# A gate chain on 32 rows, retention tiles normalised in pairs, and earlier loads in attention, in a two-layer mLSTM and retention trunk

## The chip, the cores and the metric

The kernel runs on one core of a Trainium2 chip. A core has a matrix engine (PE, with PEld for its weight loads), VectorE (DVE), ScalarE (ACT), GpSimd (POOL) and SyncE (SP), whose queue issues most DMA transfers. The metric is the device time of one execution in microseconds; lower is better.

## The reference

Two layers, each with 1024 tokens of width 1024. A layer normalises x, applies an adaptive scale and shift, projects it to queries, keys, values and gates, and runs eight heads of width 256: four mLSTM heads and four retention heads. Both kinds of head are chunked linear attention with a carried state. Cut to what matters here:

```
# mLSTM head, per chunk; li = input gate, lf = log_sigmoid(forget gate)
b = cumsum(lf);  a = b + m
g = b[:, None] - b[None, :] + li[None, :]          (causal)
m_row = max(a, max(g));  s = (q k^T) * exp(g - m_row)
h = (s v + exp(a - m_row) * C q) / max(|den|, exp(-m_row))
# retention head: s = (q k^T) * gamma^(t-s);  o = s v + gamma^(t+1) q R
# both: per-head layer norm over 256 columns, gates, y @ w_out, residual
```

The gate chain is the part that makes cumulative sums b, a running maximum of li - b, and sums of these, for every head and token, before any mLSTM head runs. Running sums and maxima restart in each layer and go over all 1024 tokens.

## The kernel before, in words

Products are made from split operands (a high part rounded to the matrix engine's fp32r format and a low part), three matmuls for one (`mm3`, lines 177 to 179 of the profile). Projections run as a list of slots: pairs of blocks in a Strassen-like scheme, with weights fetched by a `Feeder` seven or eight slots ahead into a ring of twelve tiles `R`, split by `high` (L403, ACT) and `low` (L408, POOL or DVE). Value products have 256-column matmuls, the others 512.

Beside the slots run generators, in ticks: one tick per slot (or per half block in the units before them). `launch(gen, delay)` starts a generator, and what it yields is the number of ticks until its next part. A tick only sets the place of instructions in the program. PE's order is the program's order (`manual_schedule`). The other engines' order is made by a scheduler that simulates the program in time; instructions marked `late` keep their program order among themselves. In the gate chain all DVE calls are marked so.

The gate chain (`gate_chain`) starts one tick after the gate projection. Before, it works on rows 0 to 3 (forget gate, four heads) and 32 to 35 (input gate), in two halves of 512 tokens, one after the other, with the last column of a half as the start of the next. ACT makes |f|, exp and ln; then 12 ticks; then DVE makes log-sigmoid, splits it into a coarse and a fine part, scans both (`bq`, `br`), and scans the maximum (`mx`). It collects four results in rows 0, 32, 64 and 96 of a tile `T4`; eight 128x128 transposes by PE (L562) and two copies give the column form `COL`. The maxima also go to DRAM (`mdr`), from where attention later loads decay rows, broadcast over the partitions. The chain takes the tiles `q`, `kc`, `dm`, `nd`, `cf`, `n`, `zt`, `cH`, `cL`, which attention and the rotary tables also use. `load_rotary` (L968) loads two sine tables into `dm`, with a buffer ring of two, and one into `nd`.

Attention (`attention`) handles one head in four chunks j of 256 tokens. `TABLE` gives one step for each tick: `q0` and `k0` load queries and keys of chunk 0 from DRAM into tiles `acc` (a ring of twelve, which nearly everything else uses too), `Q0` and `K0` split them (ACT L868, POOL L869), `d0` loads the decay rows of an mLSTM head into `dm` (ring of two), `m0` turns them into weights (POOL L1021, ACT L1022), `t0` loads key rows (four transfers, L905), `s0` splits them, `v0` loads values into `ring`, `S0` makes scores (L1032, then DVE L1048 to L1062, ACT L1070 for `sH`, POOL L1071 for `sL`), `V001` makes outputs of tiles 0 and 1 of chunk 0 (L1114 at chunk 0, L1123 for later chunks), and `U01` updates the state (L1091, L1094, L1096). At step 22 the next head may start.

After `values` (V), `normalise` makes the layer norm of a head. For mLSTM it runs once per chunk. For retention it runs, before, once for each V step: `V001` covers both tiles, but chunks 1 to 3 have two V steps, so each tile has its own statistics (L1160, L1161), added epsilon (L1174), power -0.5 on POOL (L1175), `nmu` (L1178) and scaling on ACT (L1180). `finish` then transposes both tiles into `zt` (L1188, one buffer) and stores them (L1193). Retention's unnormalised outputs are copied into `n` (L1144, one buffer).

Of the kernel before, what the change touches and what calls it, by code (L numbers as in the profile page):

```python
# [87 lines left out]
def tile_hybrid_trunk(ctx, tc, x, xt, c, positions, w_ada, b_ada, norm_g, w_in, w_blk, w_val, conv_w, conv_b,  # L88
# [27 lines left out]
    def ps_a():  # L116
        return pa.tile([P, 512], F32, tag="a", name=nm("pa"))
# [88 lines left out]
           for l in range(DEPTH)]  # L206
    gbd = [dpool.tile([P, HALF], F32, name=f"gbd{i}") for i in range(2)]
    mdr = [dpool.tile([NH, T], F32, name=f"mdr{l}") for l in range(DEPTH)]

    ring = [cst.tile([P, 4 * 258], F32R, tag=f"ring{i}", name=f"ring{i}") for i in range(2)]  # L210
    ring3 = [r.rearrange("p (a c) -> p a c", a=4) for r in ring]
# [291 lines left out]
    def gate_chain(l, pgs, gt):  # L503
        V = Later()
        bg = cols[l][1]
        COL = wt("COL", 8 * 16, 1)
        C4 = COL.rearrange("p (t k h) -> p t k h", t=8, k=4)
        prev = {}
        on4 = ones.to_broadcast([P, 512])
        lfs, lis_, es = [], [], []  # L510
        mxs, fbs, lif = wt("q", 1024, 2), wt("q", 1024, 2), wt("kc", 1024, 1)
        for half in range(2):
            pg = pgs[half]
            hs = slice(half * HALF, (half + 1) * HALF)
            fb, li, e = fbs[:, hs], lif[:, hs], wt("dm", 512, 2)
            A.activation(fb[0:4], pg[0:4, :], AF.Identity, bias=bg[0:4, :])
            A.activation(li[32:36], pg[32:36, :], AF.Identity, bias=bg[32:36, :])
            A.activation(e[0:4], fb[0:4], AF.Abs)
            A.activation(e[0:4], e[0:4], AF.Exp, scale=-1.0)
            lfs.append(fb)  # L520
            lis_.append(li)
            es.append(e)
        for half in range(2):
            A.activation(es[half][0:4], es[half][0:4], AF.Ln, bias=ones[0:4, 0:1])
        yield 12
        T4s = []
        for half in range(2):
            lf, li, e = lfs[half], lis_[half], es[half]
            lfq = (wt("cf", 516, 1) if half else wt("nd", 516, 1))[:, 0:512]
            V.scalar_tensor_tensor(lf[0:4], lf[0:4], 0.0, e[0:4], ALU.min, ALU.subtract)  # L530
            V.tensor_scalar(lfq[0:4], lf[0:4], MAG_Q, -MAG_Q, ALU.add, ALU.add)
            V.tensor_tensor(lf[0:4], lf[0:4], lfq[0:4], ALU.subtract)
            bq, br = e, wt("zt", 512, 1) if half else wt("n", 512, 1)
            yield 1
            V.tensor_tensor_scan(bq[0:4], on4[0:4], lfq[0:4], prev.get("bq", 0.0), ALU.mult, ALU.add)
            V.tensor_tensor_scan(br[0:4], on4[0:4], lf[0:4], prev.get("br", 0.0), ALU.mult, ALU.add)
            yield 1
            lir, T4, mx = li, wt("cL" if half else "cH", 516, 1)[:, 0:512], mxs[:, half * HALF:(half + 1) * HALF]
            liq, uh = lf, lfq
            V.tensor_scalar(liq[0:4], li[32:36], MAG_Q, -MAG_Q, ALU.add, ALU.add)  # L540
            V.tensor_copy(lir[0:4], li[32:36])
            V.tensor_tensor(lir[0:4], lir[0:4], liq[0:4], ALU.subtract)
            G.memset(T4, 0.0)
            V.tensor_tensor(uh[0:4], liq[0:4], bq[0:4], ALU.subtract)
            yield 1
            V.tensor_copy(T4[0:4], uh[0:4])
            V.tensor_tensor(T4[32:36], lir[0:4], br[0:4], ALU.subtract)
            V.tensor_tensor_scan(mx[0:4], on4[0:4], uh[0:4], prev.get("mx", 0.0), ALU.mult, ALU.max)
            yield 1
            V.tensor_copy(T4[64:68], mx[0:4])  # L550
            V.tensor_tensor(uh[0:4], bq[0:4], mx[0:4], ALU.add)
            V.tensor_tensor(T4[96:100], uh[0:4], br[0:4], ALU.add)
            Q.dma_start(mdr[l][:, half * HALF:(half + 1) * HALF], mx[0:4])
            prev = {"bq": bq[0:4, 511:512], "br": br[0:4, 511:512], "mx": mx[0:4, 511:512]}
            T4s.append(T4)
            yield 1
        yield 3
        for half in range(2):
            T4 = T4s[half]
            pt = ps_a()  # L560
            for i in range(4):
                PE.transpose(pt[:, i * P:(i + 1) * P], T4[:, i * P:(i + 1) * P], ident)  # L562
            V.tensor_copy(C4[:, half * 4:(half + 1) * 4],
                          pt.rearrange("p (t k h) -> p t k h", t=4, k=4)[:, :, :, 0:4])
# [24 lines left out]
        V.tensor_tensor(we, we, eul4[:, :, 0:6, 0], ALU.mult)  # L589
        gt.update(C4=C4, eul4=eul4, em3=em3, wi=wi, we=we, dc=dc)  # L590
# [372 lines left out]
    def load_rotary(rot):  # L963
        for which in range(2):
            for i in range(2):
# [3 lines left out]
                rot[which].append(t[:, 0:HALF])  # L969

    busy = [False]
    TABLE = ("q0 k0 d0 t0", "", "v0", "Q0 K0 m0 d1", "s0 k1", "S0", "m1 q1 K1", "v1", "Q1", "V001 t1", "S1 k2 q2", "U01",
             "s1 d2 K2", "v2 Q2", "V10 U2 m2", "S2", "t2 d3", "V11 U3 k3", "s2 q3", "v3 K3", "Q3 m3", "V20 U4",
             "S3", "", "V21 U5", "", "", "", "V30", "V31", "")
    RELEASE = 22

    def attention(l, hg, gt):
# [120 lines left out]
        def values(j, tts):  # L1098
# [6 lines left out]
            src = {}  # L1105
# [10 lines left out]
            for tt in tts:  # L1116
# [23 lines left out]
                    else:  # L1140
                        A.copy(nd3[:, tt, 0:W], po[:, 0:W])
                else:
                    src[tt] = nrm[j][:, tt, :]
                    A.copy(src[tt], po[:, 0:HD])  # L1144
            if not ml:
                launch(normalise(j, tts, src), 1)
            elif tts[-1] == 1:
                launch(normalise(j, (0, 1), [nd3[:, tt, 0:HD] for tt in range(2)]), 1)

        def gather(nd, po):  # L1150
            V.tensor_tensor(nd, po, nd, ALU.add)
            return
            yield

        def normalise(j, tts, src):
            n, a, b = len(tts), tts[0], tts[-1] + 1
            st6 = wt("st6", 12, 2)
            mv3 = wt("mv", 4, 2).rearrange("p (a b) -> p a b", a=2)
            for tt in tts:
                V.bn_stats(st6[:, 6 * tt:6 * tt + 6], src[tt])  # L1160
                V.bn_aggr(mv3[:, tt, :], st6[:, 6 * tt:6 * tt + 6])  # L1161
            va = wt("va", 2, 2)[:, 0:n]
            rs = wt("rsd", 2, 2)[:, 0:n]
            if ml:
                den = st["nd"][:, :, HD]
                r = wt("qd", 2, 2)
# [4 lines left out]
                G.tensor_tensor(rs, va, mhalf[:, 0:2], ALU.pow)  # L1171
            else:
                e = C_EPS + 2 * h + place(2 * j + a)
                V.tensor_tensor(va, mv3[:, a:b, 1], kc[:, e:e + n], ALU.add)  # L1174
                G.tensor_tensor(rs, va, mhalf[:, 0:n], ALU.pow)  # L1175
            yield 1
            nmu = wt("nmu", 2, 2)[:, 0:n]
            late(V.scalar_tensor_tensor(nmu, mv3[:, a:b, 0], -1.0, rs, ALU.mult, ALU.mult))  # L1178
            for i, tt in enumerate(tts):
                late(A.activation(nrm[j][:, tt, :], src[tt], AF.Identity, scale=rs[:, i:i + 1], bias=nmu[:, i:i + 1]))  # L1180
            if tts[-1] == 1:
                yield 1
                yield from finish(j)

        def finish(j):
            half = j // 2
# [530 lines left out]
```

## Time and profile before

| | before |
|---|---|
| median of 3 runs | 2268.21 us (2267.9 to 2268.85) |
| profiled execution | 2268.18 us |
| its span, first to last instruction | 2266.5 us |
| mean granted clock of the matrix engine | 0.979 |
| PE busy | 2151.5 us, 95% |
| DVE busy | 1817.5 us, 80% |
| ACT busy | 1159.4 us, 51% |
| POOL busy | 964.3 us, 43% |

The profile is one execution. Busy time of an engine is the time in which it had an instruction at work; for PE the matmuls overlap, so busy is not the same as full use. A wait is told as who waited, for whom, the total, how often, and the longest. The chain of waits is followed back from the last instruction, at each step to what released it. "Granted clock" is the share of full speed that PE's throttle gave.

### The profile page before, as it was taken

The page shows a single profiled execution, that of the slowest core. Times are in us where ns is not written, and L with a number is a line of the kernel's source. Part 1 is how long each engine was busy: PE and PEld are TensorE (multiplying, and loading weights), DVE is VectorE, ACT ScalarE, POOL GpSimd, SP SyncE. Part 2 cuts the span into 40 slices and gives each one's busy share as a digit, 9 for nine tenths or more (in the row PEclk, how much of TensorE's full clock was granted, in tenths as well). Part 3 has the DMA queues.
Part 4 walks back from the last instruction along what each step waited for, and adds up shares of the span by engine and source line. Part 5 has one row for each costly group of instructions (what it writes and reads, how often), then busy time and mean ns, then how long its engine had stood idle before and what let it go on. Part 6 is the DMA issues. An engine that isn't in the chain of part 4 may idle for free.

```text
span 2266.5 us, 35156 instructions
## 1 busy us (share of the span) xinstructions
PE 2151.5 (95%) x11483; PEld 1832.0 (81%) x11483; DVE 1817.5 (80%) x3205; ACT 1159.4 (51%) x2163; POOL 964.3 (43%) x842
## 2 busy tenths in 40 slices
PE   7988999999999999999999799999999899999998
PEld 5787789878898878788778678988987888788886
DVE  6899888989979998784738989788797889977653
ACT  7634345444565656553555434543565565655442
POOL 1443244445454454424366235544544453442313
PEclk9999999999999999999999899999999999999999
DMA  8266688787686777686633767776866686686974
GB/s 285 61 176 186 188 230 249 215 235 202 185 247 175 194 203 186 175 270 210 225 107 84 214 185 210 214 198 185 245 166 192 175 238 186 173 216 203 261 245 118
DMA packets 452549, 448.31 MB, mean 198 GB/s; under 512 B 191219, under 2 KB 309755, under 8 KB 452365
## 3 DMA queue, kind: packets, MB, share of 16 engines
q1 hardware_dynamic: 432636, 410.14, 58.9%
q0 software_dynamic: 19584, 35.66, 10.4%
q8 instruction: 90, 1.47, 0.3%
q14 instruction: 95, 0.77, 0.1%
q10 hardware_dynamic: 144, 0.26, 0.0%
HBM read 322.69 MB, written 123.24 MB: 197 GB/s over the span
## 4 chain that ended last, share of the span: by engine, by line
PE 57%; DVE 22%; DMA 10%; issue 5%; POOL 2%; ACT 2%; SPq 1%; DVEq 0%; POOLq 0%; ACTq 0%
PE px L177 8%; PE px L178 8%; PE px L179 8%; PE pz L179 6%; PE pz L178 6%; PE pz L177 6%; PE pa L177 4%; PE pa L179 4%; PE pa L178 4%; DVE acc L881 3%; DVE R L408 2%; PE pa L1123 2%; DVE acc L626 2%; DMA acc<-kfr 1%; PE pa L1032 1%
## 5 line engine op out<-in xcount | busy, mean ns | idle before, releaser
L403 ACT CAST wH<-R 128x512 fp32r<-128x512 f32 x616 | 377.2, 617 | 476.6 <-PE px L178 133.0
L408 POOL TENSOR_TENSOR R<-R,wH 128x512 fp32r<-128x512 f32 x276 | 397.5, 1447 | 479.5 <-ACT wH L403 325.9
L177 PE MATMUL px<-b,wH 128*128 128x512 f32 x912 | 364.8, 400 | 8.2 <-ACT acc L767 7.4
L179 PE MATMUL px<-b,R 128*128 128x512 f32 x912 | 365.7, 401 | 0.0
L178 PE MATMUL px<-b,wH 128*128 128x512 f32 x912 | 364.8, 400 | 0.0
L408 DVE TENSOR_TENSOR R<-R,wH 128x512 fp32r<-128x512 f32 x340 | 257.2, 760 | 90.5 <-ACT wH L403 87.5
L178 PE MATMUL pz<-b,wH 128*128 128x512 f32 x704 | 280.2, 398 | 1.3 <-DVE b L1262 1.3
L179 PE MATMUL pz<-b,R 128*128 128x512 f32 x704 | 281.0, 399 | 0.0
L177 PE MATMUL pz<-b,wH 128*128 128x512 f32 x704 | 279.8, 397 | 0.2 <-ACT acc L767 0.2
L177 PEld LDWEIGHTS px<-b,wH 128*128 128x128 f32 x912 | 174.6, 191 | 48.1 <-ACT acc L767 8.9
L179 PEld LDWEIGHTS px<-b,R 128*128 128x128 f32 x912 | 174.0, 191 | 42.0 <-POOL R L408 0.8
L178 PEld LDWEIGHTS px<-b,wH 128*128 128x128 f32 x912 | 174.4, 191 | 39.3
L177 PE MATMUL px<-wH,b 128*128 128x256 f32 (+1 forms) x576 | 177.7, 309 | 27.4 <-DVE acc L824 12.3
L178 PE MATMUL px<-R,b 128*128 128x256 f32 (+1 forms) x576 | 174.9, 304 | 3.7 <-DVE R L408 3.7
L179 PE MATMUL px<-wH,b 128*128 128x256 f32 (+1 forms) x576 | 175.8, 305 | 0.0
L701 POOL DMA_DIRECT2D R<-in_w_blk_dram x104 | 92.1, 886 | 185.3 <-DMA R<-in_w_blk_dram 90.8
L178 PEld LDWEIGHTS pz<-b,wH 128*128 128x128 f32 x704 | 133.5, 190 | 32.0 <-DVE b L1262 2.2
L179 PEld LDWEIGHTS pz<-b,R 128*128 128x128 f32 x704 | 133.3, 189 | 31.5
L177 PEld LDWEIGHTS pz<-b,wH 128*128 128x128 f32 x704 | 133.8, 190 | 29.4 <-ACT acc L767 0.6
L177 PEld LDWEIGHTS px<-wH,b 128*128 128x128 f32 x576 | 115.5, 201 | 32.2 <-ACT acc L817 10.4
L179 PE MATMUL pz<-wH,b 128*128 128x256 f32 (+1 forms) x448 | 134.0, 299 | 0.4 <-DVE b L1262 0.4
L177 PE MATMUL pz<-wH,b 128*128 128x256 f32 (+1 forms) x448 | 134.0, 299 | 0.0
(357 smaller groups left out, 5346.7 us busy)
## 6 DMA issues: line engine op xcount, KB each, us to landing
R<-in_w_blk_dram SPq DMA_DIRECT2D x276, 256.0 KB
vdr<-acc SPq DMA_DIRECT2D x128, 256.0 KB
ring<-vdr SPq DMA_DIRECT2D x64, 512.0 KB
R<-in_w_out_dram SPq DMA_DIRECT2D x128, 256.0 KB
R<-in_w_blk_dram POOLq DMA_DIRECT2D x104, 256.0 KB, 4.7
R<-in_w_val_dram SPq DMA_DIRECT2D x80, 256.0 KB
gdr<-acc SPq DMA_DIRECT2D x64, 256.0 KB
acc<-in_w_ada_dram SPq DMA_DIRECT2D x64, 256.0 KB
```

The lines of the kernel that those rows point to most:

```text
L177: PE.matmul(o, lt[0], rt[0], start=start, stop=False, skip_group_check=more)
L178: PE.matmul(o, lt[0], rt[1], start=False, stop=False, skip_group_check=more)
L179: PE.matmul(o, lt[1], rt[0], start=False, stop=stop, skip_group_check=more)
L403: A.copy(h, r)
L408: eng.tensor_tensor(lo, r, f(h), ALU.subtract)
L626: V.tensor_tensor(t, f(pair[0]), f(pair[1]), ALU.add)
L701: G.dma_start(raw[n], src, accum_op=ALU.add)
L881: V.scalar_tensor_tensor(acc[:, e:], pt[:, o + e - d:o + HALF - d], wcol, acc[:, e:], ALU.mult, ALU.add)
L1032: PE.matmul(pd, piece(kx[j], i, dt, tt * P, P), qd, start=dt == 0 and i == 0, stop=dt == 1 and i == 1)
L1123: PE.matmul(pi[:, 0:W], piece(qs[j], i, dt, tt * P, P), state[part][:, dt, 0:W], start=part + dt + i == 0, stop=ml and part + dt == 2)
```

## The change

There are three edits.

1. The gate chain. The raw gates (4 rows of 1024) are stored to DRAM (`gtd`) and loaded again as 32 rows (4 heads x 8 blocks) of 128 tokens. The scans run on all blocks at once. Block totals are then combined across rows: the sums by two one-column matmuls with a 32x32 triangular mask, the maxima by a PE transpose to one row, a short scan with a reset per head, and a matmul back to a column. Four transposes of 32x128 and one copy give `COL`. The `mdr` store is one transfer instead of two. The yields between the parts are new.
2. Retention tiles. `values` copies each tile into `n` as before, and `normalise` is launched once, after the second tile, for both kinds of head; the one-column operations become two-column ones.
3. Loads in attention. In `TABLE`, `k1` moves from step 4 to 3, `q1` from 6 to 5, `k2` from 10 to 9, `k3` from 17 to 16, `q3` from 18 to 17, `d2` from 12 to 8 and `d3` from 16 to 13. `q2` stays. The steps that use them stay.

```diff
-        for half in range(2):
-            ...   # two halves of 512 columns on 4 rows, as above
+        raw = wt("kc", 1024, 1)
+        for half in range(2):
+            for r in (0, 32):
+                A.activation(raw[r:r + 4, half * HALF:(half + 1) * HALF], pgs[half][r:r + 4, :], AF.Identity,
+                             bias=bg[r:r + 4, :])
+        for i in range(2):
+            Q.dma_start(gtd[l][i], raw[32 * i:32 * i + 4, :])
+        ...   # tiles in two "q" buffers, triangular mask on POOL, three small memsets
+        yield 3
+        for i, t in enumerate((fb, li)):
+            Q.dma_start(t, gtd[l][i].rearrange("h (b t) -> (h b) t", t=P))
+        yield 3
+        A.activation(e, fb, AF.Abs)
+        A.activation(e, e, AF.Exp, scale=-1.0)
+        A.activation(e, e, AF.Ln, bias=ones[0:32, 0:1])
+        yield 2
+        ...   # seven DVE operations on 32x128: log-sigmoid, its split, two scans, the input gate's split
+        yield 3
+        pc = ps_a()
+        for i, b in enumerate((bq, br)):
+            PE.matmul(pc[0:32, i:i + 1], lower, b[:, P - 1:P], start=True, stop=True)
+        ...   # carries added to bq and br, u, v, scan of the maximum
+        yield 3
+        pm = ps_a()
+        PE.transpose(pm[0:1, 0:32], mx[:, P - 1:P], ident[0:32, 0:32])
+        ...   # scan over the 32 block maxima, shifted by one
+        yield 3
+        pb = ps_a()
+        PE.matmul(pb[0:32, 0:1], exc[0:1, :], ones[0:1, 0:1], start=True, stop=True)
+        ...   # mx, s = bq + mx + br
+        yield 2
+        Q.dma_start(mdr[l].rearrange("h (b t) -> (h b) t", t=P), mx)
+        yield 2
+        pt = ps_a()
+        for i, t in enumerate((u, v, mx, s)):
+            PE.transpose(pt[:, i * 32:(i + 1) * 32], t, ident[0:32, 0:32])
+        V.tensor_copy(C4, pt[:, 0:P].rearrange("p (k h t) -> p t k h", k=4, h=4))
...
-    TABLE = ("q0 k0 d0 t0", "", "v0", "Q0 K0 m0 d1", "s0 k1", "S0", "m1 q1 K1", "v1", "Q1", "V001 t1", "S1 k2 q2", "U01",
-             "s1 d2 K2", "v2 Q2", "V10 U2 m2", "S2", "t2 d3", "V11 U3 k3", "s2 q3", "v3 K3", "Q3 m3", "V20 U4",
+    TABLE = ("q0 k0 d0 t0", "", "v0", "Q0 K0 m0 d1 k1", "s0", "S0 q1", "m1 K1", "v1", "Q1 d2", "V001 t1 k2", "S1 q2", "U01",
+             "s1 K2", "v2 Q2 d3", "V10 U2 m2", "S2", "t2 k3", "V11 U3 q3", "s2", "v3 K3", "Q3 m3", "V20 U4",
              "S3", "", "V21 U5", "", "", "", "V30", "V31", "")
...
-            if not ml:
-                launch(normalise(j, tts, src), 1)
-            elif tts[-1] == 1:
-                launch(normalise(j, (0, 1), [nd3[:, tt, 0:HD] for tt in range(2)]), 1)
+            if tts[-1] == 1:
+                launch(normalise(j, [nrm[j][:, tt, 0:HD] for tt in range(2)]), 1)
```

More of the change, by code (lines that the diff above doesn't have):

```diff
@@ L208, in tile_hybrid_trunk @@
     mdr = [dpool.tile([NH, T], F32, name=f"mdr{l}") for l in range(DEPTH)]
+    gtd = [dpool.tile([2, NH, T], F32, name=f"gtd{l}") for l in range(DEPTH)]
     ring = [cst.tile([P, 4 * 258], F32R, tag=f"ring{i}", name=f"ring{i}") for i in range(2)]
@@ L507, in gate_chain @@
         C4 = COL.rearrange("p (t k h) -> p t k h", t=8, k=4)
[L508 to L511, printed above, removed]
+        raw = wt("kc", 1024, 1)
         for half in range(2):
[L513 to L522, printed above, removed]
@@ L523, in gate_chain @@
-        for half in range(2):
[L524 to L556, printed above, removed]
@@ L557, in gate_chain @@
-        yield 3
[L558 to L564, printed above, removed]
+            for r in (0, 32):
+                A.activation(raw[r:r + 4, half * HALF:(half + 1) * HALF], pgs[half][r:r + 4, :], AF.Identity,
+                             bias=bg[r:r + 4, :])
@@ new lines, in gate_chain @@
+        for i in range(2):
+            Q.dma_start(gtd[l][i], raw[32 * i:32 * i + 4, :])
+        one, two = (wt("q", 1024, 2) for _ in range(2))
+        e, bq, br, fb, lfq, lir, tmp, small = (one[0:32, i * P:(i + 1) * P] for i in range(8))
+        u, v, mx, s, li, liq = (two[0:32, i * P:(i + 1) * P] for i in range(6))
+        lower, inc, exc, first = (small[:, i * 32:(i + 1) * 32] for i in range(4))
+        carry = two[0:32, 6 * P:6 * P + 4]
+        on = ones[0:32].to_broadcast([32, P])
@@ new lines, in gate_chain @@
+        G.memset(lower, 1.0)
+        l3 = lower.rearrange("p (h t) -> p h t", h=4)
+        G.affine_select(l3, l3, [[-8, 4], [0, 8]], ALU.is_ge, 0.0, base=0, channel_multiplier=1)
+        G.affine_select(lower, lower, [[1, 32]], ALU.is_ge, 0.0, base=-1, channel_multiplier=-1)
+        nc.vector.memset(first, 1.0)
+        nc.vector.memset(first.rearrange("p (h t) -> p h t", h=4)[:, :, 0:1], 0.0)
+        nc.vector.memset(exc, 0.0)
+        yield 3
+        for i, t in enumerate((fb, li)):
+            Q.dma_start(t, gtd[l][i].rearrange("h (b t) -> (h b) t", t=P))
@@ new lines, in gate_chain @@
+        yield 3
[3 more added lines that the diff above has]
+        yield 2
+        V.scalar_tensor_tensor(fb, fb, 0.0, e, ALU.min, ALU.subtract)
+        V.tensor_scalar(lfq, fb, MAG_Q, -MAG_Q, ALU.add, ALU.add)
+        V.tensor_tensor(fb, fb, lfq, ALU.subtract)
+        V.tensor_tensor_scan(bq, on, lfq, 0.0, ALU.mult, ALU.add)
+        V.tensor_tensor_scan(br, on, fb, 0.0, ALU.mult, ALU.add)
+        V.tensor_scalar(liq, li, MAG_Q, -MAG_Q, ALU.add, ALU.add)
@@ new lines, in gate_chain @@
+        V.tensor_tensor(lir, li, liq, ALU.subtract)
+        yield 3
+        pc = ps_a()
+        for i, b in enumerate((bq, br)):
+            PE.matmul(pc[0:32, i:i + 1], lower, b[:, P - 1:P], start=True, stop=True)
+        V.tensor_copy(carry[:, 0:2], pc[0:32, 0:2])
+        for i, b in enumerate((bq, br)):
+            V.tensor_scalar(b, b, carry[:, i:i + 1], None, ALU.add)
+        V.tensor_tensor(u, liq, bq, ALU.subtract)
+        V.tensor_tensor_scan(mx, on, u, 0.0, ALU.mult, ALU.max)
@@ new lines, in gate_chain @@
+        V.tensor_tensor(v, lir, br, ALU.subtract)
+        yield 3
+        pm = ps_a()
+        PE.transpose(pm[0:1, 0:32], mx[:, P - 1:P], ident[0:32, 0:32])
+        V.tensor_tensor_scan(inc[0:1], first[0:1], pm[0:1, 0:32], 0.0, ALU.mult, ALU.max)
+        V.tensor_tensor(exc[0:1, 1:32], inc[0:1, 0:31], first[0:1, 1:32], ALU.mult)
+        yield 3
+        pb = ps_a()
+        PE.matmul(pb[0:32, 0:1], exc[0:1, :], ones[0:1, 0:1], start=True, stop=True)
+        V.tensor_copy(carry[:, 2:3], pb[0:32, 0:1])
@@ L565, in gate_chain @@
+        V.tensor_scalar(mx, mx, carry[:, 2:3], None, ALU.max)
+        V.tensor_tensor(s, bq, mx, ALU.add)
+        V.tensor_tensor(s, s, br, ALU.add)
+        yield 2
[5 more added lines that the diff above has]
+        V.tensor_copy(C4, pt[:, 0:P].rearrange("p (k h t) -> p t k h", k=4, h=4))
         ME = wt("ME", 32, 1)
@@ L1104, in values @@
             nd3 = st["nd"]
-            src = {}
             ahead = {}
@@ L1142, in values @@
                 else:
-                    src[tt] = nrm[j][:, tt, :]
-                    A.copy(src[tt], po[:, 0:HD])
-            if not ml:
-                launch(normalise(j, tts, src), 1)
-            elif tts[-1] == 1:
-                launch(normalise(j, (0, 1), [nd3[:, tt, 0:HD] for tt in range(2)]), 1)
+                    A.copy(nrm[j][:, tt, :], po[:, 0:HD])
+            if tts[-1] == 1:
+                launch(normalise(j, [nrm[j][:, tt, 0:HD] for tt in range(2)]), 1)
         def gather(nd, po):
@@ L1153, in gather, with normalise @@
             yield
-        def normalise(j, tts, src):
-            n, a, b = len(tts), tts[0], tts[-1] + 1
+        def normalise(j, src):
             st6 = wt("st6", 12, 2)
             mv3 = wt("mv", 4, 2).rearrange("p (a b) -> p a b", a=2)
-            for tt in tts:
+            for tt in range(2):
                 V.bn_stats(st6[:, 6 * tt:6 * tt + 6], src[tt])
                 V.bn_aggr(mv3[:, tt, :], st6[:, 6 * tt:6 * tt + 6])
-            va = wt("va", 2, 2)[:, 0:n]
-            rs = wt("rsd", 2, 2)[:, 0:n]
+            va = wt("va", 2, 2)
+            rs = wt("rsd", 2, 2)
             if ml:
@@ L1170, in normalise @@
                 V.tensor_tensor(va, va, mv3[:, :, 1], ALU.add)
-                G.tensor_tensor(rs, va, mhalf[:, 0:2], ALU.pow)
             else:
-                e = C_EPS + 2 * h + place(2 * j + a)
-                V.tensor_tensor(va, mv3[:, a:b, 1], kc[:, e:e + n], ALU.add)
-                G.tensor_tensor(rs, va, mhalf[:, 0:n], ALU.pow)
-            yield 1
[L1177 to L1183, printed above, removed]
+                e = C_EPS + 2 * h
+                if j in WHOLE:
+                    V.tensor_tensor(va, mv3[:, :, 1], kc[:, e:e + 2], ALU.add)
+                else:
+                    V.tensor_scalar(va, mv3[:, :, 1], kc[:, e:e + 1], None, ALU.add)
+            G.tensor_tensor(rs, va, mhalf[:, 0:2], ALU.pow)
+            yield 1
+            nmu = wt("nmu", 2, 2)
+            late(V.scalar_tensor_tensor(nmu, mv3[:, :, 0], -1.0, rs, ALU.mult, ALU.mult))
+            for tt in range(2):
+                late(A.activation(nrm[j][:, tt, :], src[tt], AF.Identity, scale=rs[:, tt:tt + 1], bias=nmu[:, tt:tt + 1]))
+            yield 1
+            yield from finish(j)
         def finish(j):
```

## The prediction

> **What bounds the kernel.** I read the page first, then the waits of the matrix engine (PE) in windows around the edits, then busy time by windows, the chain of waits, and the queue of SP.
>
> ```profile
> span 2266.5 us, 35156 instructions
> ...
> PE 2151.5 (95%) x11483; PEld 1832.0 (81%) x11483; DVE 1817.5 (80%) x3205; ACT 1159.4 (51%) x2163; POOL 964.3 (43%) x842
> ```
>
> PE is busy for 2151.5 of 2266.5 us. No matmul of a projection, of the scores or of the values goes away with this change, so all it can win is PE's idle time, 115 us in all, and the slow stretches that follow idle time. Its price is thus read stop by stop: which wait of PE does each edit shorten, and which does it add? First the stretches of the gate chain, layer 0 (155 to 220 us) and layer 1 (1290 to 1310 us); the columns are total, count and longest.
>
> ```profile
> PE pa L562 <- DVE cL L144: 4.4, 1, 4.4
> PE px L177 <- ACT acc L817: 2.1, 2, 1.1
> ```
> ```profile
> PE pa L345 <- ACT wH L868: 4.0, 1, 4.0
> PE pa L562 <- DVE cL L144: 3.0, 1, 3.0
> ```
>
> L562 is the chain's own end: PE, which follows program order, stands at the transposes until VectorE (DVE) has made the last row of T4. Then attention's stops in three places (485 to 500, 572 to 582, 1550 to 1562 us):
>
> ```profile
> PE pa L1114 <- ACT sH L1070: 3.4, 1, 3.4
> PE pa L1114 <- POOL sL L1071: 1.2, 1, 1.2
> ```
> ```profile
> PE pa L1114 <- ACT sH L1070: 1.8, 1, 1.8
> ```
> ```profile
> PE pa L177 <- ACT n L1144: 4.6, 1, 4.6
> ```
>
> And what a stop costs beyond itself: windows right behind stops, then one undisturbed window. The columns are the window, its length, busy time and count of PE, PEld, DVE, ACT and POOL, the granted clock, DMA share and GB/s.
>
> ```profile
> 180.00:184.00 4.00, 4.00 (x20) 4.00 (x19) 3.42 (x11) 0.00 (x0) 0.00 (x0) 0.50 0.63 223
> 495.00:500.00 5.00, 4.46 (x12) 3.68 (x13) 2.67 (x7) 0.74 (x2) 3.11 (x4) 0.50 0.95 300
> 580.00:584.00 4.00, 4.00 (x12) 3.33 (x13) 2.49 (x6) 2.09 (x4) 2.81 (x3) 0.57 0.94 262
> 1304.00:1307.50 3.50, 3.46 (x9) 2.27 (x10) 3.42 (x6) 2.38 (x6) 2.44 (x3) 0.56 0.30 50
> 1310.00:1315.00 5.00, 5.00 (x23) 4.02 (x22) 1.87 (x3) 1.73 (x3) 1.35 (x2) 1.00 0.98 252
> 1562.00:1567.00 5.00, 5.00 (x17) 4.04 (x16) 4.97 (x9) 2.84 (x7) 5.00 (x6) 0.55 0.59 150
> ```
>
> After a stop the granted clock is 0.50 to 0.57 for some microseconds; busy PE time times one minus that clock is lost as well. The undisturbed window also sets the length of a tick, the unit in which the kernel's generators yield: 23 matmuls of 512 columns in 5.00 us, 0.217 us each, so 12 of them (one tick of a pair product) take 2.6 us, and "yield 3" is 7.8 us.
>
> **The gate chain: what goes.** In layer 1 the window from the chain's first DVE instruction to its last COL copy, counting the lines of the deferred DVE calls alone, holds exactly this chain; beside it, one 128-column operation of attention's scores (duration min, median, max in ns).
>
> ```profile
> 1256.30:1299.20 42.90, 24.35 (x32) 0.90 0.74 206
> ```
> ```profile
> L1051 DVE TENSOR_TENSOR acc<-acc x32: 268/282/1375, 305.5 to 2061.6; 128x128 f32<-128x128 f32 x32
> ```
>
> 32 instructions, 24.35 us. On 32 rows of 128 columns the diff has 20 (7 before the first matmuls, 6 up to the block maxima, 2 on the 32 maxima, 4 for the carry and the sums, one copy into COL) and three small memsets. At the 0.28 us median of the L1051 row, 20 make 5.6 us: about 19 us less DVE in each layer. The bounds are 0 (row length does not matter) and 24; I take 19, because L1051 is the same kind of operation at the same length. What becomes of that on PE: the L562 stops end (4.4 + 3.0); the 2.1 us at L817 are PSUM banks not drained in time and held behind DVE, and I count them as gone. The 4.0 us at L345 have another cause, seen in ScalarE's timeline (ACT):
>
> ```profile
> 1299.94 1.28 ACT L968 ACT_TABLE_LOAD   x1 [4.13 <-DMA dm<-rdr]
> ```
>
> The rotary table's load into `dm` could start only when the old chain let go of `dm` (its `e` and `bq`), and PE's operand `wH` stood behind it on ACT. The new chain holds only `q`, `kc` and COL, so this goes. Sum of stops 4.4 + 2.1 + 4.0 + 3.0 = 13.5 us. Clock: 4.00 x 0.50 = 2.0 in layer 0, 3.46 x 0.44 = 1.5 in layer 1. Together 17.0 us.
>
> **The gate chain: what comes.** PE stops for the chain at four places instead of two (carry sums, transpose of the maxima, their broadcast, final transposes); its own instructions are eight small ones for eight transposes, counted at nothing. Three places a layer lead to new waits, each with 7.8 us of yield and two to seven short DVE operations ahead of it. Queued behind a PE stop are the value products, and behind those everything. Bounds for each: 0 and the 4.4 us of the old stop; I take 1.0, nearer to the lower end since 7 x 0.28 = 2.0 us of DVE work meet 7.8 us. Six stops: +6. The new trip through `gtd` adds two stores and two loads to SP's queue and one wait of ACT (`e <- fb`) for a load; behind that wait on ACT stand the bank copies that PE needs. Each half of the trip has 7.8 us. Two transfers from the chain of waits, a larger and a smaller one, bound it:
>
> ```profile
> 152.48 7.28 DMA vdr<-acc
> ```
> ```profile
> 187.35 1.73 DMA rdr<-acc
> ```
>
> Even 7.28 is inside 7.8, the rows are small, and I take 0; if SP is late by several us it costs up to 4 us a layer. ACT itself gets 7 gate instructions for 10 and POOL loses two memsets of 128x512 for three small ones: nothing. Gate part: -17 + 6 = -11.
>
> **Attention's loads.** k1, q1, k2, k3 and q3 move one step (2.6 us) ahead, q2 stays, d2 moves four steps, d3 three. What the loads now cost on ACT, in the waits of the whole trace:
>
> ```profile
> ACT kc L868 <- DMA acc<-kfr: 72.3, 33, 7.4
> ...
> ACT q L868 <- DMA acc<-qdr: 45.5, 24, 5.1
> ```
>
> ACT holds `sH` and the bank copies behind such a cast, POOL holds `sL` behind the split. The chain of waits shows both:
>
> ```profile
> 487.59 4.04 DMA acc<-qdr
> ...
> 492.36 1.04 POOL q L869
> ...
> 494.51 0.99 POOL sL L1071
> ```
> ```profile
> 1554.22 0.45 SPq L905
> ...
> 1554.72 5.48 DMA acc<-kfr
> ```
>
> The first ends at the L1114 stops of 3.4 + 1.2, the second at the 4.6 of L1144's copy; the 1.8 stop follows a key load too. Sum 11.0 us; clock 4.46 x 0.50 + 4.00 x 0.43 + 5.00 x 0.45 = 2.2 + 1.7 + 2.2 = 6.1. A load of 4.04 or 5.48, mean 4.8, asked 2.6 sooner, is late by 46% of what it was: I take 54% of 17.1, -9. The Trainium skill (TensorE: Matmul & The Clock Gate, Part 1) has the clock fall after about one idle window of 3.4 us; by that the 1.8 us stop would cost no clock, and this term would be -8. The trace disagrees: 0.57 stands behind that stop, so its row is used.
>
> Cost of moving: k1 passes one tick of SP's queue, d2 passes t1's four key-row loads, k2 and q2; d3 passes t2's four and the next value products. An issue is 0.45 us (L905), so what is passed is delayed by 0.5 to 0.9. Two SP waits could grow:
>
> ```profile
> SPq L991 <- DVE acc L886: 7.2, 2, 4.8
> ```
> ```profile
> SPq L1013 <- DVE acc L1060: 19.5, 9, 8.9
> ```
>
> The first is a key or query load waiting for an `acc` buffer (twelve rotate), the second a decay-row load waiting for the scores to release `dm`. Behind them on SP queue the weights, which the feeder asks for seven slots ahead, 18 us; that is the cover. I take 0 for both, and 0 for decay rows as a gain; bounds -4 and +9 (eight mLSTM heads, half of the 2.2 us mean of the L1013 row).
>
> **Retention in pairs.** 48 one-column adds and 48 `nmu` become two-column ones, 24 fewer of each (and of the POOL powers):
>
> ```profile
> L1174 DVE TENSOR_TENSOR va<-mv,kc 128x1 f32<-128x1 f32 x48 | 21.9, 456 | 0.7
> ...
> L1178 DVE SCALAR_TENSOR_TENSOR nmu<-mv,rsd 128x1 f32<-128x1 f32 x48 | 21.0, 437 | 9.3 <-POOL rsd L1175 9.1
> ```
>
> 24 x 0.893 = 21 us of DVE, spread over 480 us and more. Against it, the first tile's statistics and its scaling now follow the second tile's copy, so `zt` comes later by roughly one such pair, which matters where the next copy into `n` waits for it:
>
> ```profile
> ACT n L1144 <- DVE zt L1188: 12.1, 6, 3.8
> ```
>
> Six waits that may each grow by about 1 us on ACT, against 21 us off DVE: I take -1; bounds -4 and +6.
>
> **Sum.** -11 - 9 - 1 = -21. The profiled execution took 2268.18 us (span 2266.5 and 1.7 around it), equal to the median of 2268.21 within 0.1; 2268.2 - 21 = 2247.
>
> **Rivals.** (1) Only the gate part pays: the loads are asked sooner but SP still reaches them late, held by DVE. For it: the 19.5 us of L1013, and the load at 1554 sits behind L905's four issues, which the new order leaves ahead of k2. Against: 57 late casts. 2268 - 11 = 2257. (2) The change does nothing for PE: the freed DVE time goes to waits for transfers, and other stops take the old ones' place; 2265. (3) Slower: the new PE stops. At L562 DVE was 3.0 to 4.4 us late after a chain that began with a yield of 12; if DVE is still that late, each of the three new stops a layer ends like the old one, 3.7 us mean and 1.75 us mean of clock, 6 x 5.45 = 33, instead of the +6 counted; and the two old stops stay (7.4 + 3.5). With the attention terms: 2268 + 33 - 6.1 (L817, L345) - 10 = 2285. It passes the old time from stops of about 2.7 us each with their clock ((6.1 + 10)/6), that is, when DVE's lag is over 7.8 + 2.7 = 10.5 us. For it: L562 itself; against: 19 us less DVE work in the same stretch.
>
> **Chances.** Forecast 0.54, own range 2238 to 2256 (new stops 0 to 2 us each, half to all of the load term); (1) 0.14; (2) 0.08; (3) 0.24, spread from 2273 to 2295. A measurement of this kernel can tell about 0.2%, 4.5 us. Faster 0.68, same 0.08, slower 0.24. With about one in ten outside at each end: 2227 (all the listed stops gone, and more DVE slack) to 2282.
>
> **What would show it.** Right: L562's successors and L345 without stops over 1 us; the deferred DVE work of a layer's chain near 6 us; ACT's waits for `kfr` and `qdr` (72.3 and 45.5) about halved; PE idle below 100 us. Wrong: PE stops at the new matmuls, ACT waiting for `gtd`, SP waits on L1013 grown, or PE's idle time the same in other places.

## The result

| | before | after |
|---|---|---|
| median | 2268.21 us (5 runs, 2263.56 to 2269.47) | 2254.27 us (5 runs, 2248.73 to 2261.32) |
| ratio | | 0.9945, 95% interval 0.9921 to 0.9968 |
| profiled execution, its span | 2268.18, 2266.5 us | 2248.73, 2247.0 us |
| mean granted clock | 0.979 | 0.983 |
| PE idle (span less busy) | 115.0 us | 102.9 us |

The change takes 14 us off where 21 were forecast. The profiled execution of after is the fastest of its five, 5.5 us under their median, so a difference between two traces is only read where it is larger than that or shows in several kernels.

The page of the profile after:

```profile
span 2247.0 us, 35032 instructions
...
PE 2144.1 (95%) x11489; PEld 1829.3 (81%) x11489; DVE 1779.6 (79%) x3139; ACT 1144.7 (51%) x2151; POOL 948.4 (42%) x820
```

PE's idle time fell by 12.1 us and its busy time by 7.4 (2151.5 to 2144.1), with the same matmuls but for the chain's own: fewer stops, and less time at a low clock behind them (mean 0.979 to 0.983). (From here on, line numbers differ in kernels with the new chain. From line 207 to the chain they stand 1 higher, so L408 is L409; behind it mostly 8 higher, so L824 is L832, L1070 is L1078 and L767 is L775; later ones a little less, so L1114 is L1121 and L1144 is L1150.)

**The gate chain's stretches.** The waits of PE in layer 0 (100 to 230 us), first before, then after:

```profile
PE px L177 <- DVE acc L824: 7.4, 1, 7.4
PE pa L562 <- DVE cL L144: 4.4, 1, 4.4
PE px L177 <- ACT acc L817: 2.1, 2, 1.1
PE px L178 <- DVE R L408: 1.9, 2, 1.5
```
```profile
PE px L178 <- DVE R L409: 5.4, 1, 5.4
PE pa L556 <- DVE q L144: 3.0, 1, 3.0
PE px L177 <- DVE acc L832: 2.7, 2, 1.8
PE pa L547 <- DVE q L144: 2.6, 1, 2.6
```

And in layer 1, before (1225 to 1310 us), then after (1200 to 1290 us):

```profile
PE px L177 <- DVE acc L824: 4.9, 1, 4.9
PE pa L345 <- ACT wH L868: 4.0, 1, 4.0
PE pa L562 <- DVE cL L144: 3.0, 1, 3.0
PE px L178 <- DVE R L408: 1.8, 1, 1.8
```
```profile
PE pa L547 <- DVE q L144: 9.4, 2, 8.4
PE px L178 <- DVE R L409: 1.9, 1, 1.9
```

The four stops of the forecast are gone, the stop at the final transposes included. With them the largest of the old stops, L824's 7.4 and 4.9, shrank to 2.7 and nothing; the prediction had not counted those. Nor had it counted one that ends just behind the window above, at 230.1 us of the kernel before (214 to 236 us): PE waits for a bank that ScalarE copies, and ScalarE in turn for VectorE.

```profile
PE px L177 <- ACT acc L767: 5.4, 1, 5.4
```
```profile
229.50 0.58 ACT L767 COPY acc<-px 128x512 f32<-128x512 f32 x1 [3.25 <-DVE acc L307]
```

After has 0.8 us of waits there. This stop is what turns layer 0 into a gain. The matmuls of L177 to L179 come in the same sequence in both kernels, so their start times can be compared one by one: at the matmul that the kernel before starts at 148 us, after is 7.8 us behind; at 220 us it is still 0.6 behind; at 238 us it is 6.2 ahead. Over layer 1's stretch (1240 to 1320 us of the kernel before) its lead grows by another 5.9 us.

In place of the old stops PE now stands at the carry matmuls (L547) for 12.0 us over both layers. VectorE's own order in layer 1 shows why (start, duration, idle time ahead in brackets):

```profile
1226.81 3.48 DVE L634 TENSOR_TENSOR acc<-b,b 128x512 f32<-128x512 f32 x2
1230.22 1.75 DVE L802 TENSOR_TENSOR acc<-acc,acc 128x512 fp32r<-128x512 f32 x1
1231.88 1.28 DVE L634 TENSOR_TENSOR acc<-b,b 128x512 f32<-128x512 f32 x2
1233.09 0.68 DVE L655 SCALAR_TENSOR_TENSOR acc<-acc,acc 128x512 f32<-128x512 f32 x1
1233.69 0.27 DVE L144 SCALAR_TENSOR_TENSOR q<-q 32x128 f32<-32x128 f32 x1
```

The chain's first operation (1233.69) starts four us after PE had come to a stand (1229.7), with no idle time on DVE ahead of it. Its input had been ready for 31 us, since ScalarE's logarithm:

```profile
1202.20 0.40 ACT L535 ACTIVATE q<-q,ones 32x128 f32<-32x128 f32 x1
```

So it was not the new trip through `gtd` that held the chain, but its place in DVE's order. Busy time by windows just there, with the columns as in the prediction:

```profile
1205.00:1230.00 25.00, 22.80 (x176) 22.37 (x174) 24.76 (x24) 12.24 (x24) 19.14 (x13) 0.93 0.37 106
1230.00:1238.00 8.00, 0.00 (x0) 0.00 (x0) 7.96 (x12) 4.34 (x7) 5.71 (x5) 0.64 0.62 171
```

DVE is busy for 24.76 of the 25 us before the stop. A short chain placed behind a full queue is still late.

**Attention.** ScalarE's waits for keys and queries after, against 72.3 and 45.5 before:

```profile
ACT kc L876 <- DMA acc<-kfr: 70.3, 28, 7.3
ACT q L876 <- DMA acc<-qdr: 51.4, 28, 4.5
```

Loads asked a step sooner left these waits where they were.

### The profile page after: what moved, and what is told of

Same layout as the page of the kernel before. It is cut to its first block, busy times and chain, and to the rows that moved or that the text cites. A ratio compares the mean times of both kernels' runs of the same rounds, so it can differ in the third digit from the quotient of the medians.

```text
span 2247.0 us, 35032 instructions
## 1 busy us (share of the span) xinstructions
PE 2144.1 (95%) x11489; PEld 1829.3 (81%) x11489; DVE 1779.6 (79%) x3139; ACT 1144.7 (51%) x2151; POOL 948.4 (42%) x820
## 5 line engine op out<-in xcount | busy, mean ns | idle before, releaser
L409 POOL TENSOR_TENSOR R<-R,wH 128x512 fp32r<-128x512 f32 x276 | 391.9, 1425 | 478.8 <-ACT wH L404 354.1
L177 PE MATMUL px<-b,wH 128*128 128x512 f32 x912 | 361.8, 397 | 2.9 <-ACT acc L775 2.5
L179 PE MATMUL px<-b,R 128*128 128x512 f32 x912 | 363.1, 398 | 0.0
L409 DVE TENSOR_TENSOR R<-R,wH 128x512 fp32r<-128x512 f32 x340 | 260.0, 768 | 92.2 <-ACT wH L404 85.7
L179 PE MATMUL pz<-b,R 128*128 128x512 f32 x704 | 280.0, 398 | 0.0
L177 PE MATMUL pz<-b,wH 128*128 128x512 f32 x704 | 279.0, 396 | 0.0
L177 PEld LDWEIGHTS px<-b,wH 128*128 128x128 f32 x912 | 173.0, 190 | 41.7 <-ACT acc L775 3.5
L179 PEld LDWEIGHTS px<-b,R 128*128 128x128 f32 x912 | 172.3, 189 | 40.6
L177 PE MATMUL px<-wH,b 128*128 128x256 f32 (+1 forms) x576 | 179.6, 312 | 16.9 <-ACT acc L825 7.9
L179 PE MATMUL px<-wH,b 128*128 128x256 f32 (+1 forms) x576 | 177.2, 308 | 0.0
L179 PEld LDWEIGHTS pz<-b,R 128*128 128x128 f32 x704 | 132.8, 189 | 31.2
L177 PEld LDWEIGHTS pz<-b,wH 128*128 128x128 f32 x704 | 133.3, 189 | 28.6 <-issue 0.2
L877 POOL TENSOR_TENSOR kc<-acc,kc 128x512 fp32r<-128x512 f32 x64 | 90.6, 1416 | 123.3 <-ACT kc L876 104.5
L177 PEld LDWEIGHTS px<-wH,b 128*128 128x128 f32 x576 | 116.9, 203 | 22.0 <-ACT acc L825 8.9
L177 PE MATMUL pz<-wH,b 128*128 128x256 f32 (+1 forms) x448 | 134.4, 300 | 0.0
```

Of the source, the lines that this page charges most:

```text
L177: PE.matmul(o, lt[0], rt[0], start=start, stop=False, skip_group_check=more)
L179: PE.matmul(o, lt[1], rt[0], start=False, stop=stop, skip_group_check=more)
L409: eng.tensor_tensor(lo, r, f(h), ALU.subtract)
L877: eng.tensor_tensor(dst[1], src, f(dst[0]), ALU.subtract)
```

## The experiments

All times are medians, each against the kernel before as timed beside it (2267.8, 2268.1 and 2270.0 us). Ratios have 95% intervals.

| kernel | us | ratio |
|---|---|---|
| gate_only | 2253.27 | 0.9940 (0.9908 to 0.9972) |
| table_only | 2278.68 | 1.0048 (1.0031 to 1.0065) |
| pairs_only | 2262.58 | 0.9981 (0.9964 to 0.9998) |
| late_carry | 2247.86 | 0.9917 (0.9893 to 0.9940) |
| no_table | 2243.67 | 0.9887 (0.9867 to 0.9908) |
| no_table_late | 2239.06 | 0.9874 (0.9853 to 0.9895) |
| d_only | 2269.77 | 1.0011 (0.9993 to 1.0029) |
| table_held | 2295.91 | 1.0119 (1.0098 to 1.0139) |
| k12_moved | 2247.03 | 0.9900 (0.9874 to 0.9925) |
| q13_k3_moved | 2257.60 | 0.9948 (0.9930 to 0.9966) |
| acc_eleven | 2250.91 | 0.9935 (0.9908 to 0.9961) |
| later_loads | 2252.12 | 0.9920 (0.9898 to 0.9943) |

**One part at a time.** Theory A in the expectations is the prediction's own sum; B has the gate chain carry nearly everything; C has only the sorting of the instructions count. Three kernels each have one of the three edits (as numbered under the change) on top of the kernel before: the first in gate_only, the second in pairs_only, the third in table_only.

> The kernel before with the gate chain on 32 rows alone. Theory A (the prediction's terms, each edit by itself): about -11 us, 2257. Theory B (the two traces: all stretches of the gate chain end 14.6 us sooner, attention 5 us): the gate chain carries nearly all of the measured -14, so 2254 to 2256, with PE's stops at L547 (8.4 + 2.6 us in the trace after) in it as well. Theory C (the three edits only re-sort the order of the other engines, and the gain is such a re-sorting): within 4 us of before.

> The kernel before with the moved steps of the TABLE alone. Theory A: -9 us, 2259, with ACT's waits for kfr and qdr (72.3 and 45.5 us before) about halved. Theory B: 0 to -3 us, ACT's waits for kfr and qdr unchanged as in the trace after (70.3 and 51.4), since SP is late for another reason than its place in the order. Theory C: anything within 5 us either way.

> The kernel before with retention normalised once for two tiles alone. Theory A: -1 us (DVE about 21 us less busy, hidden). Theory B: 0. If the later transpose into zt holds the next copy into n more than before (12.1 us in 6 waits), it is slower by up to 6 us.

The gate chain alone takes 14.5 us off (0.60%), the pairs 5.2 (0.19%), and the new TABLE alone adds 10.9 us (0.48%), against -9 forecast. A and B are both wrong on it, and so is C, which allowed 5 us either way. Its waits, for kfr and qdr:

```profile
ACT kc L868 <- DMA acc<-kfr: 69.3, 25, 6.7
ACT q L868 <- DMA acc<-qdr: 45.6, 26, 4.6
```

**More ticks ahead of the carry matmuls**, on the changed kernel:

```diff
         V.tensor_tensor(lir, li, liq, ALU.subtract)
-        yield 3
+        yield 8
         pc = ps_a()
```

> The changed kernel with 8 ticks instead of 3 ahead of the carry matmuls (L547). If PE's stops there (8.4 + 1.1 us in layer 1, 2.6 in layer 0, and the slow clock behind them, 13.7 us at half) are the price of the new chain, they go and the kernel is 10 to 15 us faster than after, about 2240 to 2244. If DVE is only late because the whole stretch is bound by DVE, the same idle time comes back at the next stop (L832, L409) and the time stays at 2254.

The stops at L547 went, and the median is 6.4 us under the changed kernel's, though the two intervals overlap. Not all of the 12 us came back as time: PE's waits in layer 0 and layer 1 (100 to 200 and 1200 to 1270 us) show what was next late:

```profile
PE px L177 <- DVE acc L832: 9.6, 2, 5.8
PE px L178 <- DVE R L409: 5.4, 1, 5.4
```
```profile
PE px L177 <- DVE acc L832: 6.5, 1, 6.5
```

L832 is the old L824: a bank that DVE has still to read. The stop follows DVE's full queue from one PE instruction to another.

**The old TABLE with the rest of the change**, without and with the eight ticks; the edit is the TABLE of the kernel before.

> The changed kernel with the old TABLE: gate chain and pairs alone. If the parts measured singly add up (0.9940 x 0.9981 = 0.9921), the time is 2250, some 18 us under the kernel before, and under the changed kernel (0.9945) by 5 us. If the moved loads cost nothing once the gate chain is short (they cost 0.48% alone, but 0.9940 x 0.9981 x 1.0048 = 0.9969 is more than the changed kernel's 0.9945), it is equal to the changed kernel: 2254 to 2256. If only the sorting of the instructions counts, anywhere within 2245 to 2262 with ScalarE's waits for keys and queries (70.3 and 51.4 us) as they were.

> The same with eight ticks, in place of three, ahead of the carry matmuls (L547). Additive: the eight ticks took 0.28% off the changed kernel (0.9945 to 0.9917), so 0.9921 - 0.0028 = 0.9893, 2243 to 2245, with no stop at L547. If what is won there comes back at the same places of the attention's begin (L832 stops of 3 to 6 us), 2247 to 2250.

Without the moved loads the other two edits give 0.9887, and its interval lies wholly under that of the changed kernel: the loads cost 0.58% (10.6 us at the medians) in this company too. The eight ticks add 4.6 us at the medians, which the intervals don't separate; no_table_late is the fastest kernel of the case, 29 us under before and 15 under after. That gate and pairs together (1.13%) give more than their single gains (0.60 and 0.19) is within the width of the intervals, and stays open.

**Which loads, and through what.** Decay rows alone (d2, d3), and the new TABLE with ScalarE's casts kept in program order:

```diff
# d_only: d2 at step 8, d3 at step 13, the rest of TABLE as before
# table_held: the new TABLE and
-                split_to((t[:, 0:512], t[:, 512:1024]), raw)
+                late(A.copy(t[:, 0:512], raw))
+                G.tensor_tensor(t[:, 512:1024], raw, f(t[:, 0:512]), ALU.subtract)
```

> The kernel before with only the decay rows' loads moved (d2 from step 12 to 8, d3 from 16 to 13). If the moved decay rows are what makes the new TABLE slower (SyncE waits for dm, L1013, 18.2 to 24.1 us, and weights queue behind), it is +8 to +11 us, 2276 to 2279, with SyncE's waits on L1013 at 24 us. If the moved keys and queries are, it is within 3 us of the kernel before, 2265 to 2271. If only the sorting counts, no telling: up to 8 us either way with waits alike.

> The kernel before with the new TABLE, and ScalarE's casts of queries and keys (L868) kept in program order among the deferred instructions, so that the planner cannot put them ahead. Theory of the cast that follows its load: in the traces the loads were asked 2.5 to 4 us sooner, but the casts of q1, q3 and k3 moved up by 2.5 to 4.5 us as well (median from cast to scores: q1 9.7 to 14.2 us, k3 12.3 to 14.7, q3 7.8 to 11.0), so ScalarE waits as before. Held back, the waits for keys and queries (69.3 + 45.6 us with the new TABLE) fall below 80 us together and the time comes to 2259 to 2268. If the loss comes from decay rows or the queue of SyncE, the waits may fall but the time stays at 2275 to 2281. If casts held back are late for VectorE's and GpSimd's work, it is slower still, over 2281.

The decay rows cost nothing that can be told from none (SyncE's wait of L1013 for L1049 stays at 18.2 us), so keys and queries carry the loss. With the casts held, ScalarE's waits for these loads all but vanish (in this kernel L999 is the line of the held cast):

```profile
ACT q L999 <- DMA acc<-qdr: 4.0, 2, 2.1
...
ACT kc L999 <- DMA acc<-kfr: 3.2, 3, 1.4
```

7.2 us, against 114.9 with the new TABLE alone, and the kernel is 17 us slower than that. So a shorter wait for loads is not by itself a gain, and the gain that the expectation gave the held casts is refuted. The experiment does two things at once, though: the queries' casts now stand 4 to 6 us ahead of the scores and the keys' 4 to 13 (before 8 to 15 and 8 to 16, medians by chunk), which is late, and a load's buffer is held twice as long (issue to the end of the split: 1976 us in sum, 1045 before).

The next four runs take these apart. On the base of no_table: only k1 and k2 moved; only q1, k3 and q3; eleven `acc` buffers for twelve; and, on no_table_late, the five loads one step later than in the kernel before.

```diff
# k12_moved: k1 at step 3, k2 at step 9, the rest as before
# q13_k3_moved: q1 at step 5, k3 at step 16, q3 at step 17, the rest as before
# acc_eleven
-NACC = 12
+NACC = 11
# later_loads: k1 at step 5, q1 at 7, k2 at 11, k3 at 18, q3 at 19
```

> Gate chain and pairs with the old TABLE (2244 before), and only k1 and k2 asked a step sooner. All the TABLE's moves cost 10.6 us there (2254.3 against 2243.7). Casts of k1 and k2 did not move with their loads (16.3 to 16.4 and 16.5 to 16.4 us ahead of the scores), so here the only thing that grows is the time for which a load holds an acc buffer (k1, issue to the end of the split: 7.9 to 10.1 us). Theory of the held buffer: this part carries the cost, 2251 to 2255. Theory of the cast that follows its load into ScalarE's and GpSimd's order: this part costs nothing, 2240 to 2247. If only the sorting counts: anywhere from 2238 to 2252, with no tie to the other part.

> The same base, and only q1, k3 and q3 asked a step sooner. Their casts moved up with them (by 4.5, 2.5 and 3.2 us) and their buffers are held no longer. Theory of the held buffer: 2240 to 2247. Theory of the cast that follows its load: this part carries the cost, 2250 to 2255, with ScalarE's sH standing longer for VectorE (sH waits for L1059 and L1070 from 20 to 27 us or more). If only the sorting counts: 2238 to 2252.

> Gate chain and pairs with the old TABLE, and eleven acc buffers for twelve. Theory of the held buffer: the ring is tight, so a buffer less costs at least what the moved loads cost, 2252 to 2270, with SyncE and ScalarE waiting longer for acc. Theory of the cast that follows its load: the ring has slack for it, 2240 to 2249.

> Gate chain and pairs with eight ticks ahead of the carry matmuls (2239.06 before), and k1, q1, k2, k3 and q3 asked one step later than in the kernel before, the other way from the change. If lateness of loads is on the path, as the prediction had it, this costs 9 us: 2246 to 2250. Theory of the cast that follows its load: the casts move back by a step too, ScalarE and GpSimd come sooner to what PE waits for, and it gains or is equal: 2231 to 2240. Theory of the held buffer: holds stay as they are, 2237 to 2242.

q1, k3 and q3 carry the cost (0.9948 against 0.9887, intervals apart), k1 and k2 none that shows (0.9900). This is the prediction of the cast that follows its load. The traces say what it displaces. In head 9 of after, ScalarE's timeline in chunk 2, then the same head in no_table:

```profile
1479.87 0.37 ACT L1150 COPY n<-pa 128x256 f32<-128x256 f32 x1 [0.16 <-PE pa L179]
1487.50 0.62 ACT L876 CAST kc<-acc 128x512 fp32r<-128x512 f32 x1 [7.26 <-DMA acc<-kfr]
1488.24 0.62 ACT L876 CAST q<-acc 128x512 fp32r<-128x512 f32 x1
1488.76 0.40 ACT L1078 CAST sH<-acc 128x256 fp32r<-128x256 f32 x1
```
```profile
1480.99 0.37 ACT L1150 COPY n<-pa 128x256 f32<-128x256 f32 x1 [0.17 <-PE pa L179]
1482.42 0.41 ACT L1078 CAST sH<-acc 128x256 fp32r<-128x256 f32 x1 [1.05 <-DVE acc L1070]
1486.25 0.62 ACT L876 CAST kc<-acc 128x512 fp32r<-128x512 f32 x1 [3.42 <-DMA acc<-kfr]
```

In no_table `sH` is cast first, then the next keys. In after the keys' cast of chunk 3, and the queries' with it, were planned ahead of chunk 2's `sH`, ScalarE waits 7.26 us for that load, and `sH` starts 8.9 us behind the copy of `n` where it was 1.4. The load itself was issued behind chunk 2's key rows on SyncE:

```profile
1479.94 2.65 SPq L913 DMA_DIRECT2D acc<-kdr  x4
1482.63 0.45 SPq L999 DMA_DIRECT2D acc<-kfr  x1
1483.18 0.41 SPq L999 DMA_DIRECT2D acc<-qdr  x1
```

Counted over the 16 heads of a trace, chunk 3's key cast stands ahead of chunk 2's `sH` in 12 heads in table_only, q13_k3_moved and after, and in none in before, d_only, no_table, k12_moved and later_loads. From the end of chunk 2's score matmuls to the end of its `sL` it takes 14.5, 14.7 and 14.2 us on average in the first three, and 10.7 to 11.0 in the five others. So the change of order is shown, and that it comes with the cost in every kernel. (table_held has none of it either; there the casts themselves are late.) How much of the cost is k3's and how much q1's was not separated, and head 9 itself has no PE stop over 1 us in that stretch. ScalarE's waits at `sH` for VectorE's scores, which the expectation put at 27 us or more, are 34.5 us in q13_k3_moved, but 29.9 in k12_moved, where no cost shows, so they don't tell the two apart.

One kind of PE stop does: waits for ScalarE's copies of the mLSTM outputs out of their banks (`nd`). They make 4.7 us in after, 4.8 in table_only and 2.9 in q13_k3_moved, and also 2.1 in later_loads and 8.4 in table_held; in before, d_only, no_table and k12_moved there are none. So the kernels that lose time by the places of their loads have them, and the others don't. The largest in after, ScalarE's timeline and then PE's:

```profile
922.32 0.62 ACT L876 CAST kc<-acc 128x512 fp32r<-128x512 f32 x1 [3.80 <-DMA acc<-kfr]
922.85 0.65 ACT L1148 COPY nd<-pa 128x258 f32<-128x258 f32 x2
```
```profile
923.27 0.39 PE L177 MATMUL pa<-ring,b 128*128 128x258 f32 x1 [2.20 <-ACT nd L1148]
```

Here k2's cast, which has moved with the whole TABLE, stands ahead of the copy; it waits 3.80 us for its load, and PE stands 2.20 us for the copy. In no_table the copy comes first and PE does not stop. So one stop is traced from the load to PE. Where the rest of the 10.6 us is paid stays open: executions of one kernel differ by 20 us and more.

A buffer less costs 0.48%, with intervals that just touch (0.9867 to 0.9908, 0.9908 to 0.9961), which lies between the two expectations and speaks for little slack in the `acc` ring; but k1's longer hold (10.4 us for 7.6) cost nothing to be seen. Loads a step later cost 0.46%, some 10 us (0.9920 against 0.9874, intervals apart), about the 9 that the prediction put on a step of lateness and against the gain or draw that the theory of the cast gave; the casts of all five moved back with them (q1 from 9.0 to 4.8 us ahead of the scores). So both directions cost: of the three places tried, the old one is the best.

## Why the prediction was right, and where it was not

The time came out 7 us above the forecast and inside its own range, by errors that cancel. That is luck: the term of the loads was off by 20 us, more than the whole change, and the gate chain and the pairs gave more than was counted for them.

- **Gate chain, -11.** Right in kind; -14.5 measured alone. Gone as said: L562, L817 in layer 0, L345. "Deferred DVE work near 6 us": from the first operation of layer 1 to the last sum:

```profile
1229.00:1266.00 37.00, 7.51 (x19) 0.82 0.75 226
```

  and the copy into COL is 0.28 more, 7.8 us for 20 operations where 5.6 were worked out and 24.35 stood before. What was mis-sized: the new stops. Six at 1.0 us were taken because 2.0 us of DVE work meet 7.8 us of ticks. That compared the work with the ticks and left out what is ahead of it on DVE: stops of 8.4, 1.1 and 2.6 us came at L547 and one of 3.0 at L556, none at the others, 15 us where 6 were counted. The sum also gave the new stops no clock, though it had done so for the old ones. Behind the longest it was 0.50, half of 6.64 us of busy PE:

```profile
1232.20:1245.80 13.60, 6.64 (x33) 6.54 (x34) 10.71 (x21) 4.67 (x7) 5.48 (x5) 0.50 0.85 270
```

  On the other side, the stops at L824 (12.3 us in both layers) shrank to 2.7 and the one at L767 from 5.4 to 0.8, and were in no term. So both halves of the sum were too small, and their difference came out near. Rival (3), DVE as late as ever at the new stops, was thus half there: its mechanism acts at the first of the three places in layer 1 and at the first two in layer 0, and after these the rest of the chain is in time.
- **Attention's loads, -9.** Wrong in sign: +10.9 alone, +10.6 in company. The step that failed is "a load asked 2.6 sooner is late by 46% of what it was". It took the cast's place as fixed. In the trace of table_only q1's, k3's and q3's casts moved up by 4.5, 2.5 and 3.2 us with their loads, so ScalarE waits about as long as before (117.8 us; 114.9 in table_only, 121.7 in after), and other work stands behind that wait: `sH`, and the bank copies that PE waits for. Rival (1), SyncE reaches the loads late anyway, has its piece of truth in the four key-row issues ahead of k3, but it gave zero, not a loss. The bounds of the cost of moving (-4 to +9) were put on decay rows and SyncE's waits; d_only shows no cost of that part (0.9993 to 1.0029).
- **Pairs, -1.** -5.2 at the medians, -0.5 to -8.2 by the interval; the lower bound of -4 was nearer than the value taken. The 21 us off DVE didn't come: its busy time was 1817.5 us before and 1817.7 in pairs_only. The groups of `nmu`, the two-column ones before, then all of pairs_only (count, busy time, mean ns, idle time ahead):

```profile
L1178 DVE SCALAR_TENSOR_TENSOR nmu<-mv,rsd 128x2 f32<-128x2 f32 x40 | 17.1, 428 | 15.3 <-POOL rsd L1171 13.6 <-POOL rsd L1175 1.7
```
```profile
L1175 DVE SCALAR_TENSOR_TENSOR nmu<-mv,rsd 128x2 f32<-128x2 f32 x64 | 40.3, 630 | 21.9 <-POOL rsd L1172 21.9
```

  In the mean, 88 operations of about 0.43 us (17.1 and 21.0) became 64 of 0.63. The mean is a mixture: before, 60 of the 88 took 0.15 us and 28 took 1.2 (medians); in pairs_only 34 are short and 30 long. Fewer operations meant fewer short ones, so the 0.44 and 0.46 us by which the prediction priced each were the mis-sized step. `n`'s waits for `zt`, feared to grow from 12.1 us, were 11.9. Where the 5 us come from is not shown.
- **The marks.** PE idle under 100 us: missed, 102.9. No stop over 1 us at the final transposes and at L345: right. Waits for keys and queries halved: wrong. Of the signs of being wrong, stops at the new matmuls came (15 us), ACT waited for `gtd` once, for 1.7 us, and SyncE's waits for `dm` (L1013, now L1021) grew from 37.7 to 45.8 us.

## What to carry to other kernels

A wait of an engine off the critical path is no gain to be had until it is known what stands behind it; here they could be all but taken away, at a loss. Where a planner places instructions by when their data should come, asking for data sooner also moves the consumer ahead of other work, so look at what the consumer then overtakes, and pin down its place apart from the load's. And when a chain is shortened, compare its due time with the queue ahead of it on its engine, not with its own length: here the last 25 us of that engine's busy time said more than the sum of the chain. A mean from a profile is no price for one operation until its short and long cases are told apart.

## What the runs showed of the hardware

- One DVE split of 128x512, 0.68 us in the kernel before at the same place, took 4.67 us in after while GpSimd ran three splits of the same size, and PE stood for 5.4 us behind it; a stop of 5.4 to 5.6 us is there in all nine kernels with the new chain, and none over 1.5 in the five with the old one.

```profile
102.44 4.67 DVE L409 TENSOR_TENSOR R<-R,wH 128x512 fp32r<-128x512 f32 x1
```
```profile
102.52 4.03 POOL L877 TENSOR_TENSOR b<-acc,b 128x512 fp32r<-128x512 f32 x3
```

  The Trainium skill (SBUF — State Buffer, section "SBUF: two separate sides") says that a VectorE operation with two SBUF inputs and a GpSimd operation that reads SBUF exclude each other, for a whole instruction, and that the one that starts first goes first. The trace agrees in part: the long operation ends 0.56 us after the third split, but by the records it started 0.08 us before the first of them and was held through all three. In the kernel before, VectorE's split started 0.10 us before the first of three such splits of GpSimd, and took 0.68 us. So the recorded starts do not tell which of the two cases comes, and whether GpSimd is the cause was not tried.
- Two scans of 32x128 took 2.81 us in after and 0.72 in no_table_late. In both they follow the same work, so the length of a short operation from one trace is no safe price for it in a busy stretch.
